# First half-step's entry taken from the features-on-partitions copy of x: norms by products with a column of ones

## Chip, cores and metric

The kernel runs on one core of one Trainium2 chip. The metric is the device time of one execution in microseconds (us); the median of several runs counts. TensorE is called PE (its weight loads PEld), VectorE DVE, ScalarE ACT, GpSimd POOL, and SyncE, whose queue issues most DMAs, SP.

## The reference

One decoder layer on x of 1024 tokens by 1024 features, all in float32, with a first SwiGLU half-step, a mixer (attention and pooling), a second half-step and a last norm:

```
h = x + 0.5 * swiglu(rms_norm(x, ffn1_norm), w1, w3, w2)
u = rms_norm(h, mix_norm);  proj = u @ w_in
h = h + (sigmoid(gA) * yA + sigmoid(gB) * yB) @ w_out
h = h + 0.5 * swiglu(rms_norm(h, ffn2_norm), ...)
out = rms_norm(h, final_norm)
rms_norm(x, g) = x * rsqrt(mean(x*x, axis=-1) + 1e-6) * g
swiglu(x, w1, w3, w2) = (silu(x @ w1) * (x @ w3)) @ w2
```

Only the start of the first half-step is touched: the norm of x and what is made of it for the products with w1 and w3 (1024 by 2816 each).

## The kernel before

**Products.** Each matrix product is split as Strassen and Winograd do it, with seven products of half-size blocks in place of eight. For a pair j of two 128-column strips of w1 (quad a) and of w3 (quad b), a quad runs the products m = 1, 6, 2, 7, 5, 4, 3. The normed x enters as seven operands of 512 features by 512 tokens: `b11`, `b21` (first 512 tokens, low and high features), `b22` (last tokens, high features), and four sums `t1` to `t4` of the blocks. m=1 uses b11, m=2 b21, m=6 t2, m=7 t3, m=5 t1, m=4 t4, m=3 b22. Every operand, of x and of the weights, is split into a higher part (ACT copies it to a shorter float format, fp32r) and a lower part (the difference, by DVE or POOL), and a product is 12 matmuls of 128x128 by 128x512: four blocks of features by three pairings of the parts (`Sevens.product`, L314). Weights come in 512 KB pieces (`raw`, L69) and are split by `Sevens.split` (L303 on ACT, L306 on POOL or DVE). Results leave PSUM through `a_out` and `b_out` (L473 and after).

**Operands of x.** The left operands need features on partitions. Before, x is loaded by rows, 128 tokens on partitions (`load_rows`, L769). Per row tile ACT squares and sums along the row (`squares`, L259), DVE and POOL make the inverse root (`inverse`, L263 and L264), DVE scales by it and by the gain (`scaled_part` L270, `scaled` L267), and `Rows` has PE transpose four 128x128 blocks into a PSUM bank (L381), ACT copy the higher part from it (L382) and DVE subtract for the lower part (`Rows.lower`, L385). For the last four row tiles `Entry.run` also makes t1, t2, t4 (DVE, L423 to L425) and t3 (POOL, L426) by rows and transposes all five. The gain is spread over partitions by widening it to columns (L808) and transposing (L814).

**Order.** `begin_up1` is under a manual schedule: each engine gets its instructions in the order in which the code records them. It runs 12 products, m=1 and m=2 of both quads for three pairs, first m=1 of pairs 0 and 1, while the rest of x is made ready between them; each takes its weights' split two products ahead (`operand(i + 2)`). `up` then runs m = 6, 7, 5, 4, 3 of those six quads, and after them the other pairs. `keep_on(n)` has PE multiply ones by ones into an unused bank (`idle`, L804) while it would stand. The loads of x and of the first weights share SP's queue, at most some eight in flight.

Of the kernel before, what the change touches and what calls it, by code (L numbers as in the profile page):

```python
# [126 lines left out]
def tile_block(  # L127
# [31 lines left out]
    def sbuf(name, side="left", bufs=1):  # L159
        return tc.tile_pool(name=name, bufs=bufs, side=side, reuse_waits="tile")  # L160
# [7 lines left out]
    def bank(tag, name):  # L168
        return psum.tile([P, HALF], F32, tag=tag, name=name)

    def tmp(name):
        return keep.tile([P, 1024], F32, tag="tmp", bufs=TMP_BUFS, name=name)

    def row(name):
        return keep.tile([P, 1024], F32, tag="raw", bufs=RAW_BUFS, name=name)

    def h_tile(name):
        return keep.tile([P, D], F32, tag="h", bufs=NT, name=name)
# [2 lines left out]
    consts.tile([P, 24], F32, name="pad")  # L181
    ident = consts.tile([P, P], F32, name="ident")
    ones = consts.tile([P, P], F32, name="ones")
    mhalf = consts.tile([P, 1], F32, name="mhalf")
    consts.tile([P, 32], F32, name="pad2")
    ve.memset(ones, 1.0)
    ve.memset(mhalf, -0.5)
    h = []
    h_dram = [[dram.tile([P, D], F32, name=f"h{i}_dram{t}") for t in range(NT)] for i in range(2)]

    def load_gain(src, name):
        t = keep.tile([P, D], F32, tag="gain", bufs=1, name=f"gain_{name}")
        nc.scalar.dma_start(t, src.to_broadcast([P, D]))
        return t

# [3 lines left out]
    def ffn_pieces(w1, w3, w2, ahead):  # L199


        order = [(j, w, i) for j in range(NPAIR) for w in (w1, w3) for i in range(2)]
        order.sort(key=lambda o: (o[2], o[0]) if o[0] < ahead else (2,))

        spare = lambda j, i: (h_tile,) if ahead == 3 and (j, i) == (0, 1) else ()
        raws.pieces += [(w[2 * j + i], (1024,), *spare(j, i)) for j, w, i in order]
        by = w2.rearrange("(j o p) c -> o p j c", o=2, p=P)
        for m in DOWN:
            for js in PAIRS:
                for k, n in m.loads:  # L210
                    raws.pieces.append((by[k][:, js, n * HALF:(n + 1) * HALF], (js.stop - js.start, HALF)))
# [45 lines left out]
    def squares(t, out):  # L257
        inv[t] = small.tile([P, 2], F32, tag="nst", name=f"nst_{t}")
        ac.activation(out, h[t], AF.Square, accum_out=inv[t][:, 0:1])  # L259
# [6 lines left out]
    def scaled(t, out, gain):  # L266
        ve.scalar_tensor_tensor(out, h[t], inv.pop(t)[:, 1:2], gain, op0=OP.mult, op1=OP.mult)  # L267

    def scaled_part(t, c, gain):
        ve.scalar_tensor_tensor(h[t][:, c], h[t][:, c], inv[t][:, 1:2], gain[:, c], op0=OP.mult, op1=OP.mult)  # L270

    def norm_rows(t, gain, name, alloc=row):
        y = alloc(f"hn_{name}{t}")
        squares(t, y)
# [7 lines left out]
    SUMS = ("t4", "b22", "b11", "t2", "b21", "t3", "t1")  # L282
    LOWS, HIGHS = slice(0, HALF), slice(HALF, S)

    def sums_of_x(pool, name, order, **kw):
        return {
            s: tuple(pool.tile([P, 4, HALF], F32R, name=f"x{part}_{s}_{name}", **kw) for part in ("hi", "lo"))
            for s in order
        }

    class Sevens:
# [14 lines left out]
            eng.tensor_tensor(w[:, 1], src, w[:, 0].bitcast(F32), op=OP.subtract)  # L306
            return w

        def product(self, p, w, x, start=True):
            hi, lo = self.X[x]  # L310
            for k in range(4):
                r = slice(k * P, (k + 1) * P)
                for q, (a, b) in enumerate(three((w[:, 0, r], w[:, 1, r]), (hi[:, k, :], lo[:, k, :]))):
                    pe.matmul(p, a, b, start=(start and k == 0 and q == 0), stop=(k == 3 and q == 2),  # L314
                              skip_group_check=not start)
# [3 lines left out]
    class Quad:  # L319
# [36 lines left out]
                ve.tensor_tensor(src, a12, self.s2, op=OP.subtract)  # L356
            self.w[m] = self.sv.split(src, f"{n}{m}", eng)

        def run(self, m, back=True):
            if m not in self.w:  # L360
                self.operand(m)
            w, n = self.w.pop(m), self.n
            x = {1: "b11", 2: "b21", 3: "b22", 4: "t4", 5: "t1", 6: "t2", 7: "t3"}[m]
            key = {1: "x", 2: "x", 5: "v", 3: "v"}.get(m, m)
            if m not in (2, 3):
                self.bank[key] = bank("mm" if key in ("x", "v") else "acc", f"u_{self.sv.name}{n}{m}")
            self.sv.product(self.bank[key], w, x, start=m not in (2, 3))
            if m == 3 and back:
                raws.back(2)
            return self.bank[key]  # L370
# [72 lines left out]
    class Pair:  # L443
# [3 lines left out]
        def __init__(self, sv, j, sums, early=False, spare=False):  # L447


            self.sv, self.j, self.sums = sv, j, sums  # L450
            self.place_of = [h_tile if spare else tmp, h_tile if early else tmp]
            self.u2 = (lambda n: h_tile(f"u2_{n}")[:, :HALF]) if spare else (lambda n: sv.half_tile("u", n))
            self.y = []
            self.A, self.B = Quad(sv, f"{j}a"), Quad(sv, f"{j}b")
            self.u = {}
# [303 lines left out]
    ac.activation(warm, mhalf, AF.Silu)  # L759

    scope = ExitStack()
    X = sums_of_x(scope.enter_context(sbuf("x1")), "f1", SUMS)

    for t in range(NT):
        h.append(h_tile(f"x{t}"))

    def load_rows(*ts):
        for t in ts:
            nc.sync.dma_start(h[t], x[t * P:(t + 1) * P, :])  # L769

    gain_row = keep.tile([P, D], F32, tag="gain", bufs=1, name="gain_ffn1")
    square = row("square")
    columns_tile = tmp("columns")
    columns = columns_tile.rearrange("p (k c) -> p k c", k=KT)

    def load_all():
        nc.scalar.dma_start(ident, c_ident)
        load_rows(0, 1, 2, 3)
        raws.depth = 2
        raws.load()  # L780
        load_rows(4)
        raws.depth = 3
        raws.load()
        load_rows(5)
        raws.depth = 4
        raws.load()
        load_rows(6, 7)
        raws.depth = 6
        raws.load()

    def pre_run(sv, todo, first, low):
        return Entry(sv, [(*((q.A, m, q.a_out), (q.B, m, q.b_out))[k],) for q, m in todo for k in range(2)], low,
# [2 lines left out]
    def begin_up1():  # L795


        load_all()
        idle = bank("mm", "idle")

        def keep_on(n):

            for _ in range(n):
                pe.matmul(idle[:, :P], ones, ones, start=True, stop=True)  # L804

        def widen(b):
            k = slice(4 * b, 4 * b + 4)
            ve.tensor_copy(columns[:, k], gain1[:, k, None].to_broadcast([P, 4, P]))  # L808

        def gains(b):  # L810

            p = bank("acc", f"gain{b}")
            for k in range(4):
                pe.transpose(p[:, k * P:(k + 1) * P], columns[:, 4 * b + k], ident)  # L814
            return p

        r = {}

        def rows(t, what, c):
            scaled_part(t, c, gain_row)  # L820
            r[t] = Rows(X, what, h[t][:, c], t)

        keep_on(12)
        widen(0)
        squares(0, square)
        widen(1)
        inverse(0)
        g = [gains(b) for b in range(2)]
        keep_on(2)
        ve.tensor_copy(gain_row[:, LOWS], g[0])  # L830
        squares(1, square)
        squares(2, square)
        rows(0, "b11", LOWS)
        inverse(1)
        keep_on(2)
        inverse(2)
        squares(3, square)
        rows(1, "b11", LOWS)
        r[0].lower()
        keep_on(3)  # L840
        rows(2, "b11", LOWS)
        inverse(3)
        r[1].lower()
        keep_on(3)
        pairs = [Pair(sv1, j, sums, True, j == 2) for j in range(3)]
        entry = pre_run(sv1, [(q, m) for m in (1, 2) for q in pairs[:2]] + [(pairs[2], m) for m in (1, 2)],
                        pairs[0], h[:4])
        entry.operand(0)
        rows(3, "b11", LOWS)
        r[2].lower()  # L850
        keep_on(2)
        r[3].lower()
        ve.tensor_copy(gain_row[:, HIGHS], g[1])
        entry.product(0)
        entry.operand(1)

        square2 = columns_tile
        squares(4, square2)
        for t in (0, 1):
            rows(t, "b21", HIGHS)  # L860
        entry.product(1)
        entry.out(0)
        entry.operand(2)
        entry.operand(3)
        inverse(4)
        r[0].lower()
        for t in (2, 3):
            rows(t, "b21", HIGHS)
            r[t - 1].lower()
        entry.product(2)  # L870
        entry.out(1)
        squares(5, square2)
        r[3].lower()
        entry.product(3)
        entry.operand(4)
        entry.out(2)
        entry.operand(5)
        entry.out(3)

        def high(t, part):  # L880
            if part == 0:
                inverse(t)
                return
            scaled(t, h[t], gain_row)
            return h[t]

        def after(t):
            if t + 2 < NT:
                squares(t + 2, square2)
            if t == 5:  # L890
                raws.depth = 8
                raws.load()

        entry.run(high, after, 4)
        return pairs

    sums = spilled("f1")
# [1249 lines left out]
```

## Time and profile before

| | us |
|---|---|
| median of 3 runs | 1937.25 (1936.93 to 1937.53) |
| the profiled execution | 1938.85 |
| its span, first to last instruction | 1937.1 |
| first matmul of the first product | 14.06 |
| first matmul on b21 (fifth product) | 27.86 |
| first matmul with m=6 (quad a of pair 0) | 59.68 |
| first matmul of quad b of pair 0 with m=6 | 75.05 |
| first matmul of pair 3 | 143.4 |

A line of a group or of the timeline names the engine, the line of the kernel, the operation, the tiles (out<-in) and shapes; in the timeline the first two numbers are start and duration in us, and xN means that N like instructions are merged, the duration from the first's start to the last's end. What stands in brackets is the engine's idle time before, and who ended it. In a table of stretches each engine has its busy time and (x) the number of its instructions. A matmul's recorded duration contains its pipeline's depth, so records of matmuls overlap: 12 of a product are recorded at 0.39 each and take 2.73 together.

### The profile page before, as it was taken

The numbers are of one execution on the slowest core, as the hardware profiler recorded it, in microseconds if no ns is written. First come the engines' busy times: TensorE is split into PE (matmuls) and PEld (weight loads), VectorE is DVE, ScalarE is ACT, GpSimd is POOL, SyncE is SP. The second block draws the span as 40 slices with busy tenths as digits, with TensorE's granted clock in tenths as the row PEclk, the third lists the DMA queues.
The fourth block names the chain that finished last, engine by engine and source line by source line (L and its number), as shares of the span: only waits on it lengthen the run. The fifth ranks groups of instructions, "written<-read, shape, count | busy, mean of one in ns | idle before, by whom it ended". The sixth has DMA issues, their size and how long they took to land.

```text
span 1937.1 us, 24938 instructions
## 1 busy us (share of the span) xinstructions
PE 1906.0 (98%) x8938; PEld 1574.9 (81%) x8938; DVE 1347.7 (70%) x2012; ACT 759.3 (39%) x1361; POOL 741.2 (38%) x557
## 2 busy tenths in 40 slices
PE   9999999999999999999999999999999999999997
PEld 7788888887888888888877888887888888878885
DVE  7786556658676876658775896787665566577776
ACT  6333333333344543334445762353333333333343
POOL 5433333332222355445544356543333333322231
PEclk9999999999999999999999999999999999999998
DMA  4154222336465538665668877733433233364654
GB/s 187 44 195 167 90 87 104 136 114 212 146 235 208 197 99 257 219 207 198 217 232 303 279 226 248 271 133 118 165 121 114 82 105 123 121 206 136 205 199 150
DMA packets 144796, 331.98 MB, mean 171 GB/s; under 512 B 19104, under 2 KB 39840, under 8 KB 143136
## 3 DMA queue, kind: packets, MB, share of 16 engines
q1 hardware_dynamic: 137136, 308.00, 46.4%
q10 hardware_dynamic: 7536, 22.39, 3.4%
q8 instruction: 70, 1.15, 0.3%
q14 instruction: 54, 0.44, 0.1%
HBM read 229.61 MB, written 100.73 MB: 171 GB/s over the span
## 4 chain that ended last, share of the span: by engine, by line
PE 39%; DVE 4%; issue 3%; POOL 2%; ACT 2%; DMA 1%; DVEq 0%; POOLq 0%; ACTq 0%
PE d_f L708 7%; PE wo L1870 4%; PE u_mixm L314 2%; PE yp L1626 2%; PE o L1572 1%; PE u_f210a L314 1%; PE u_f29b L314 1%; PE u_f29a L314 1%; PE u_f28b L314 1%; PE u_f28a L314 1%; PE u_f27b L314 1%; PE u_f27a L314 1%; PE u_f26b L314 1%; PE u_f26a L314 1%; PE u_f25b L314 1%
## 5 line engine op out<-in xcount | busy, mean ns | idle before, releaser
L708 PE MATMUL d_f<-bhi_f,alo_f 128*128 128x512 f32 x616 | 240.8, 391 | 2.5 <-POOL alo_f L670 2.1
L708 PE MATMUL d_f<-bhi_f,ahi_f 128*128 128x512 f32 x616 | 240.6, 391 | 0.2 <-ACT ahi_f L666 0.2
L708 PE MATMUL d_f<-blo_f,ahi_f 128*128 128x512 f32 x616 | 239.7, 389 | 0.0
L670 POOL TENSOR_TENSOR alo_f<-g_f,ahi_f 128x512 fp32r<-128x512 f32 x70 | 99.0, 1430 | 299.5 <-ACT ahi_f L666 299.5
L314 PE MATMUL u_mixm<-xhi_t_mix,wc_mixm 128*128 128x512 f32 x608 | 195.3, 392 | 1.8 <-POOL wc_mixm L306 1.7
L314 PE MATMUL u_mixm<-xhi_b_mix,wc_mixm 128*128 128x512 f32 x456 | 149.1, 392 | 1.2 <-ACT y_m L972 0.9
L708 PEld LDWEIGHTS d_f<-bhi_f,alo_f 128*128 128x128 f32 x616 | 115.6, 188 | 29.6 <-POOL alo_f L670 4.0
L314 PEld LDWEIGHTS u_mixm<-xhi_t_mix,wc_mixm 128*128 128x128 f32 x608 | 113.8, 188 | 27.3 <-POOL wc_mixm L306 3.8
L708 PEld LDWEIGHTS d_f<-bhi_f,ahi_f 128*128 128x128 f32 x616 | 115.6, 188 | 24.2 <-ACT ahi_f L666 0.6
L708 PEld LDWEIGHTS d_f<-blo_f,ahi_f 128*128 128x128 f32 x616 | 115.7, 188 | 23.8
L314 PE MATMUL u_mixm<-xlo_t_mix,wc_mixm 128*128 128x512 f32 x304 | 118.4, 390 | 0.0
L306 POOL TENSOR_TENSOR wc_mixm<-s_mixm,wc_mixm 128x512 fp32r<-128x512 f32 x52 | 74.4, 1433 | 108.1 <-ACT wc_mixm L303 104.1
L314 PEld LDWEIGHTS u_mixm<-xhi_b_mix,wc_mixm 128*128 128x128 f32 x456 | 85.6, 188 | 19.5 <-ACT y_m L972 1.3
L303 ACT ACTIVATE wc_mixm<-s_mixm 128x512 fp32r<-128x512 f32 x76 | 47.3, 629 | 126.5 <-DVE s_mixm L347 63.3
L314 PE MATMUL u_mixm<-xlo_b_mix,wc_mixm 128*128 128x512 f32 x228 | 88.8, 389 | 0.0
L666 ACT ACTIVATE ahi_f<-g_f 128x1024 fp32r<-128x1024 f32 x84 | 81.9, 975 | 4.0 <-DMA g_f<-gs_f 3.9
L306 POOL TENSOR_TENSOR wc_mixm<-raw,wc_mixm 128x512 fp32r<-128x512 f32 x40 | 61.0, 1530 | 34.6 <-ACT wc_mixm L303 32.1
L666 ACT ACTIVATE bhi_f<-s_f2w 128x512 fp32r<-128x512 f32 x55 | 32.8, 627 | 97.9 <-DVE s_f2w L686 87.0
L1870 PE MATMUL wo<-w_o,o_hi 128*128 128x512 f32 x224 | 69.3, 391 | 0.0
L666 ACT ACTIVATE bhi_f<-s_f1w 128x512 fp32r<-128x512 f32 x55 | 33.0, 630 | 86.8 <-DVE s_f1w L686 82.0
L314 PEld LDWEIGHTS u_mixm<-xlo_t_mix,wc_mixm 128*128 128x128 f32 x304 | 57.1, 188 | 11.8 <-DVE xlo_t_mix L385 0.2
L670 DVE TENSOR_TENSOR alo_f<-g_f,ahi_f 128x1024 fp32r<-128x1024 f32 x42 | 51.3, 1222 | 7.3 <-ACT ahi_f L666 7.3
(1302 smaller groups left out, 5103.8 us busy)
## 6 DMA issues: line engine op xcount, KB each, us to landing
g_f<-gs_f SPq DMA_DIRECT2D x70, 512.0 KB, 4.5
gs_f<-y_f SPq DMA_DIRECT2D x88, 256.0 KB, 3.0
raw<-in_w2a_dram SPq DMA_DIRECT2D x35, 512.0 KB, 3.7
raw<-in_w2b_dram SPq DMA_DIRECT2D x35, 512.0 KB, 4.6
gs_f<-gb_f SPq DMA_DIRECT2D x46, 256.0 KB, 2.2
raw<-in_w1a_dram SPq DMA_DIRECT2D x22, 512.0 KB, 4.8
raw<-in_w3a_dram SPq DMA_DIRECT2D x22, 512.0 KB, 5.5
raw<-in_w1b_dram SPq DMA_DIRECT2D x22, 512.0 KB, 4.3
```

The costliest lines, as they stand in the source:

```text
L303: ac.activation(w[:, 0], src, AF.Copy)
L306: eng.tensor_tensor(w[:, 1], src, w[:, 0].bitcast(F32), op=OP.subtract)
L314: pe.matmul(p, a, b, start=(start and k == 0 and q == 0), stop=(k == 3 and q == 2), skip_group_check=not start)
L666: ac.activation(hi[:, c], src, AF.Copy)
L670: eng.tensor_tensor(lo[:, d], src[:, o], hi[:, d].bitcast(F32), op=OP.subtract)
L708: pe.matmul(self.banks[m][t], l, r, start=(first and q == 0), stop=(last and q == 2))
L1572: pe.matmul(p, l, r, start=(j == 0), stop=(j == end))
L1626: pe.matmul(p, a, b, start=(j == 0), stop=(j == 11))
L1870: pe.matmul(banks[m][t], l, r, start=(st == 0 and j == 0 and q == 0), stop=(st == 1 and j == 1 and q == 2))
```

## The change

x is taken from a copy that lies in memory with features on partitions, in two halves of 512 tokens, each in four tiles of two blocks of 128 features. ACT squares such a tile (`square`), its two blocks are added (`add`: on DVE for the first half, on POOL for the second), and `count` multiplies the sum by a column of ones on PE, four products of one column, so that PSUM gathers the sum of squares with tokens on partitions. `inverses` makes the inverse roots (DVE, POOL), widens them to 128 columns on DVE, and has PE transpose them: a PSUM bank `by_token` then holds the inverse root of each of the 512 tokens on all partitions. `normed` multiplies a block by the gain (now one number per partition) and by that bank, in place. ACT copies the higher part and DVE subtracts for the lower part, both from SBUF. The sums t1 to t4 are made by blocks of features on blocks that already lie as they are used; `Rows`, `Entry.run` and their transposes are no longer used here (they stay for the later entries). Products 0 and 1 are run alternately, one block of features at a time. The squares and the widened columns use the places of operands not yet made (t4, b22, t3). One piece of weights more is loaded ahead (depth 7), and two temporary tiles of pair 2 lie elsewhere (`place_of`, `u2`).

```diff
-    X = sums_of_x(scope.enter_context(sbuf("x1")), "f1", SUMS)
...
+    x_in = [[h_tile(f"x{half}_{j}").rearrange("p (r c) -> p r c", r=2) for j in range(KT // 2)] for half in range(2)]
...
-        load_rows(0, 1, 2, 3)
...
+        load_x(0, 0, 1, 2, 3)
+        load_raws(2)
+        load_x(1, 0, 1)
+        load_raws(3)
+        load_x(1, 2)
+        load_raws(4)
+        load_x(1, 3)
+        load_raws(7)
...
+        def square(half, j):
+            ac.activation(place(half, j), x_in[half][j], AF.Square)
+
+        def add(half, j, eng):
+            t = place(half, j)
+            eng.tensor_tensor(t[:, 0], t[:, 0], t[:, 1], op=OP.add)
+
+        def count(half, j):
+
+            t = place(half, j)
+            for q in range(4):
+                pe.matmul(sums_of[half][:, q:q + 1], t[:, 0, q * P:(q + 1) * P], ones[:, 0:1],
+                          start=(j == 0 and q == 0), stop=(j == 3 and q == 3), skip_group_check=True)
+
+        def inverses(half):
+
+            st = small.tile([P, 8], F32, tag="nst8", name=f"nst_x{half}")
+            ve.tensor_scalar(st[:, :4], sums_of[half][:, :4], 1.0 / D, EPS, op0=OP.mult, op1=OP.add)
+            gp.tensor_tensor(st[:, 4:], st[:, :4], mhalf4, op=OP.pow)
+            wide = wides[half][:, 0, :].rearrange("p (q c) -> p q c", q=4)
+            ve.tensor_copy(wide, st[:, 4:, None].to_broadcast([P, 4, P]))
+            by_token[half] = bank("acc", f"inverses{half}")
+            for q in range(4):
+                pe.transpose(by_token[half][:, q * P:(q + 1) * P], wide[:, q], ident)
...
+        def normed(half, k):
+            b = block(half, k)
+            ve.scalar_tensor_tensor(b, b, gain1[:, k:k + 1], by_token[half], op0=OP.mult, op1=OP.mult)
...
+        def lower(what, k, src):
+            hi, lo = X[what]
+            ve.tensor_tensor(lo[:, k, :], src, hi[:, k, :].bitcast(F32), op=OP.subtract)
...
+        keep_on(10)
+        for j in range(4):
+            square(0, j)
+            add(0, j, ve)
+            count(0, j)
+            keep_on(2 if j < 3 else 3)
+        inverses(0)
...
+        operand(0)
+        operand(1)
+        for k in range(4):
+            split("b11", k)
+        lower("b11", 3, block(0, 3))
+        for k in range(4):
+            for i in (0, 1):
+                product(i, range(k, k + 1))
+        operand(2)
+        out(0)
+        square(1, 0)
+        add(1, 0, gp)
+        operand(3)
+        out(1)
+        square(1, 1)
+        add(1, 1, gp)
+        split("b21", 4)
+        split("b21", 5)
+        square(1, 2)
+        add(1, 2, gp)
+        split("b21", 6)
+        square(1, 3)
+        add(1, 3, gp)
+        split("b21", 7)
+        lower("b21", 3, block(0, 7))
+        product(2)
+        for j in (0, 1):
+            count(1, j)
+        out(2)
+        product(3)
+        for j in (2, 3):
+            count(1, j)
+        operand(4)
+        inverses(1)
+        operand(5)
+        out(3)
...
+        def first_sums(k):
+            normed(1, k)
+            normed(1, k + 4)
+            ve.tensor_tensor(b11(k), b12(k), b11(k), op=OP.subtract)
+            ve.tensor_tensor(t2(k), b22(k), b11(k), op=OP.subtract)
+            gp.tensor_tensor(b12(k), b22(k), b12(k), op=OP.subtract)
+            higher("t2", k, t2(k))
+            if k > 0:
+                lower("t2", k - 1, t2(k - 1))
...
+        def last_sums():
+            both("t1", b11)
+            for k in range(4):
+                ve.tensor_tensor(b21(k), t2(k), b21(k), op=OP.subtract)
+            X.update(sums_of_x(x1, "f1", ("t4",)))
+
+        beside = [lambda k=k: first_sums(k) for k in range(4)]
+        beside += [lambda: (lower("t2", 3, t2(3)), both("t3", b12)), last_sums,
+                   lambda: both("t4", b21, (0, 1)), lambda: both("t4", b21, (2, 3))]
+        for i in range(4, n):
+            product(i)
+            beside[i - 4]()
+            operand(i + 2)
+            out(i)
...
+        both("b22", b22)
```

`split(what, k)` is `normed(0, k)`, `higher`, and the lower part of the block before; `both` is higher and lower for the named blocks.

## The prediction

> **What bounds the kernel now.** I read the page first, for the engines over the whole span and the granted clock.
>
> ```profile
> span 1937.1 us, 24938 instructions
> PE 1906.0 (98%) x8938; PEld 1574.9 (81%) x8938; DVE 1347.7 (70%) x2012; ACT 759.3 (39%) x1361; POOL 741.2 (38%) x557
> PEclk9999999999999999999999999999999999999998
> ```
>
> PE is busy almost throughout at full clock, so what an entry takes or gives in PE time goes to the end undiminished. Next I cut the table of busy time by stretches at the events that the change moves: first product (14.05), first product on `b21` (27.86), first product of a quad's second part, m=6 (59.65), the same of the b-quad (75.05), start of the fourth pair (143.40).
>
> ```profile
> core 0: us, PE busy (x) PEld busy (x) DVE busy (x) ACT busy (x) POOL busy (x), PEclk, DMA share, GB/s
> 0.00:14.05 14.05, 11.10 (x72) 10.06 (x72) 6.77 (x17) 8.81 (x16) 3.33 (x9) 1.00 0.89 343
> 14.05:27.86 13.81, 13.09 (x64) 10.58 (x64) 11.58 (x16) 8.60 (x16) 7.41 (x7) 1.00 0.57 227
> 27.86:59.65 31.79, 31.47 (x177) 26.29 (x176) 27.95 (x37) 18.83 (x36) 21.17 (x15) 1.00 0.16 51
> 59.65:75.05 15.40, 14.42 (x62) 10.96 (x61) 11.32 (x15) 5.90 (x11) 5.62 (x5) 1.00 0.20 52
> 75.05:143.40 68.35, 68.35 (x302) 56.42 (x301) 55.40 (x69) 18.93 (x32) 23.28 (x17) 1.00 0.45 150
> ```
>
> The last stretch holds 25 products: 68.35 / 25 = 2.73 us each, PE never idle, DVE 81% busy. From 65 us on the list of waits has none of PE's up to 420. So the change is worth the shift of the instant 75.05, and nothing later makes up for it. In 27.86 to 59.65 DVE is 88% and POOL 67% busy: they are close behind PE. How these two get along is in the timeline:
>
> ```profile
> start us, us, engine line op out<-in xcount [idle before <-releaser]
> 25.37 0.69 DVE L423 TENSOR_TENSOR x<-x,x 128x512 f32<-128x512 f32 x1
> 25.54 1.68 POOL L306 TENSOR_TENSOR wc_f10a<-raw,wc_f10a 128x512 fp32r<-128x512 f32 x1 [1.82 <-PE u_f11a L314]
> 26.09 1.67 DVE L424 TENSOR_TENSOR s_f1t<-x,x 128x512 f32<-128x512 f32 x1
> 27.17 1.74 POOL L306 TENSOR_TENSOR wc_f10b<-raw,wc_f10b 128x512 fp32r<-128x512 f32 x1
> 27.79 1.67 DVE L425 TENSOR_TENSOR s_f1t<-s_f1t,x 128x512 f32<-128x512 f32 x1
> ...
> 33.90 2.26 POOL L306 TENSOR_TENSOR wc_f11b<-raw,wc_f11b 128x512 fp32r<-128x512 f32 x1
> 35.28 1.29 DVE L385 TENSOR_TENSOR xlo_t_f<-x_t,xhi_t_f 128x512 fp32r<-128x512 f32 x2 [0.26 <-ACT xhi_t_f L382]
> ```
>
> L424 and L425 take 0.69 us alone (as L423) and 1.67 beside POOL; POOL's 1.28 becomes 1.68 and 1.74. Each ends 0.55 (DVE) or 1.15 (POOL) after the other: they take turns. But the lower halves L385, which read PSUM, run two in 1.29 inside POOL's instruction. So a DVE operation with both inputs in SBUF costs up to 1.0 more beside POOL, one with an input in PSUM nothing.
>
> **What the change takes and adds.** Removed from PE: 112 transposes of x and 8 of gains (16 take 34.02 to 35.68, 0.10 each: about 12 us). Added: 32 products with a column of ones, 8 transposes. From ACT: 8 squares with their accumulator read (0.19) become 8 without. From DVE: 28 lower halves from PSUM become 28 with both inputs in SBUF. That is the step I price highest. Loads have equal size and places in the queues, so I take the landings of before: x at 4.4, 5.9, 7.2, 8.5 (squares start there), weights after.
>
> I lay the new order out engine by engine with these rows: product 2.73; ACT square 1.06, copy 0.52 in a row, 0.60 alone; DVE 0.61 in a row, 0.69 alone; POOL 1.28; POOL's power 0.55. A column-of-ones product is not in the trace. A 128x128 one of `idle` is two records, 0.10 each in a row, hence 0.2; if only its weights counted it could be half. I take 0.2, four make 0.8.
>
> *To product 2.* The last square ends at 9.5, add 10.2, counts 11.2, DVE and the power 12.0. The widening copy (0.38, L808) now stands beside a POOL split that begins at 12.0; no row shows a copy there. Bounds: 0.4 and, by L424, 0.4 + 1.1. I take the upper end: 13.6. The Trainium skill, SBUF — State Buffer, "Who interferes with whom", says that copies can enter a mode that holds the port pair shared with GpSimd, the other fully blocking; by it both widening copies wait, as I have them. Transposes, norm (0.74, L270), ACT copy: first product at 15.7, where 14.06 was. Its second matmul waits for the lower half, and products 0 and 1 alternate by blocks: 24 matmuls at 0.228 (2.73 / 12) and 0.5 of waiting. Product 2 starts at 21.7; before 22.54. Gain 0.8.
>
> *To product 4.* Product 2 ends at 24.4. PE then counts the second half's squares, and every later product stands behind that in its queue. Its cover in the first half was loading; here it is one chain over four engines. ACT: an eviction at 21.2, square at 21.7, weights' copy, eviction, square at 23.7; POOL: add, split, add, to 26.6; PE counts, product 3 from 27.5 to 30.2. Behind two copies of `b21` ACT squares at 25.8, and behind a third that waits for DVE at 28.4; POOL's add (delayed 0.5 by a lower half) ends at 31.3, counts 32.3, DVE 32.5. The power stands behind a split on POOL (31.3 to 33.0), so 33.5; widening copy 35.0, transposes: product 4 at 35.5, before 27.86. Loss 7.6.
>
> *To m=6.* Now DVE has, in one queue ahead of the operand of m=6: 8 norms from PSUM (0.64), 2 evictions (0.61), and with both inputs in SBUF 8 differences, 4 lower halves of t2, 4 of t3, 4 of t1, 4 differences for t4, 2 lower halves of t4, and the two sums of weights: 28 x 0.61. That is 5.1 + 1.2 + 17.1 = 23.4, and some 0.5 of dependences. POOL has 10 operations in that time (6 splits, 4 differences); with 28 of 38 DVE operations exposed about 7 meet one, at 1.0: 7. DVE ends at 35.8 + 30.9 = 66.7, ACT copies, m=6 starts at 67.4; before 59.68. The eight products between need 21.9 and wait 4.8 for weights' splits that stand on POOL behind differences and blocked turns, so they end at 62.2 and PE stands: what it saves in transposes disappears under a longer DVE queue. Loss 7.7 in all at this point.
>
> *m=6, 7, 5, 4, 3.* Before, 15.4 for 13.7 of products. After, weights are split just before use (0.9 twice before a third matmul), the lower half for m=5 stands behind four of `b22` on DVE (1.3), and m=3 waits 1.1 for its split on POOL: 13.7 + 4.2 = 17.9. The b-quad starts at 85.3; before 75.05. Laid out so, before's own rows give 75.3, so I take off 0.2: **+10.0 us**. If the two widening copies wait for nothing it is +8; if all ten POOL operations are met, +13.
>
> The profiled execution took 1938.85 (span 1937.1 and 1.75 around it): 1948.9. It lies 1.6 above the median of the runs, 1937.25, so the forecast is 1947.3.
>
> **Rivals.** *PE stays the bound (faster).* If the second half's norms and sums are ready whenever PE wants them, products 2 to 11 take 27.3 from 21.7, with 3.2 of counting (16 at 0.2) and 0.4 of transposes: m=6 at 52.6, 7.1 earlier, and 1930. For it: PE loses 12 us of work and DVE has 12% idle before. Against: it decides only if DVE's 38 operations ahead of m=6, 23.4 us even undisturbed, end by 52, so begin by 28.5, and by the chain above the second half's last square is not done before 29. Chance 0.08.
>
> *The port is no loss (same).* If DVE's operations on SBUF alone pass POOL as those from PSUM do, its queue ahead of m=6 is 24 us and begins 3 earlier (two copies at 1.1, the adds): it ends at 56.8, m=6 starts about 2 earlier than before, and the waits behind it, which stay longer, leave -1.3: 1936. L424, L425 and L267 (1.28 alone, 2.34 beside POOL) speak against. With results between that and +3.9, 0.12.
>
> *Longer still.* PE stands for 3.0 us before product 4 and 5.2 before m=6. The first 24 records of `idle`, after a standing start, took 4.81 us, 0.20 each, against 0.10 later. If the waits bring that back, some 24 records again at double cost are 2.4 each time; most would lie under the waits named above. With the worst meeting of POOL this makes +13 to +15, 1950 to 1952. The Trainium skill, TensorE: Matmul & The Clock Gate, part 1, has the clock halve after about 3.4 us without work; the second wait is longer than that, the first is not. No row of before has such a wait in mid-kernel. Chance 0.20.
>
> **Numbers.** The forecast's own case, +6 to +12.5, has 0.60. A measurement of this kernel can tell about 0.2% (3.9 us) from no change: slower 0.60 + 0.20 = 0.80, same 0.12, faster 0.08. The range takes the forecast's case, the longer one and a little of the half-hidden port: 1940 to 1953.
>
> **What would show it.** Right: PE idle ahead of the inverses' transposes of the second half by about 3 us and ahead of u_f10a m=6 by about 5; DVE over 95% busy from 36 to 66 us with lower halves of 1.6 to 1.8 us beside POOL's splits; u_f13a starting near 153 instead of 143.4; nothing changed behind it but the shift. Wrong: lower halves of 0.69 us beside POOL, PE without gaps from 16 to 60 us, or m=6 before 60 us.

## The result: 19 us slower

The changed kernel takes 1956.13 us (median of 4 runs, 1955.18 to 1956.55), the one before 1937.09 beside it: a ratio of 1.0097, 95% interval 1.008 to 1.0115. The forecast was 1947.3 with a range to 1953: the sign was right, the time lies above the range. The profiled execution took 1956.07, span 1954.3. The page of the changed kernel, engines and granted clock:

```profile
span 1954.3 us, 24784 instructions
PE 1913.3 (98%) x8886; PEld 1580.4 (81%) x8886; DVE 1356.5 (69%) x2012; ACT 759.5 (39%) x1353; POOL 746.3 (38%) x555
...
PEclk7999999999999999999999999999999999999999
```

PE has 52 matmul records fewer than before and 7.3 us more busy time, and the first slice of the clock row, 9 before, is 7. That is the first hint at what the forecast lacked. The table of stretches of the changed kernel, cut at the same events (first product, product 4, m=6, quad b of pair 0, pair 3):

```profile
core 0: us, PE busy (x) PEld busy (x) DVE busy (x) ACT busy (x) POOL busy (x), PEclk, DMA share, GB/s
0.00:20.15 20.15, 16.39 (x80) 15.48 (x81) 6.01 (x11) 7.63 (x10) 3.86 (x7) 0.69 0.92 362
20.15:44.22 24.07, 19.42 (x85) 16.04 (x85) 12.60 (x16) 12.14 (x19) 12.85 (x9) 0.78 0.07 27
44.22:76.58 32.36, 25.37 (x98) 18.94 (x96) 30.92 (x38) 13.78 (x26) 17.15 (x10) 0.92 0.05 17
76.58:95.00 18.42, 17.26 (x61) 12.96 (x62) 14.14 (x18) 8.79 (x16) 7.33 (x6) 0.83 0.22 72
95.00:163.10 68.10, 68.10 (x301) 56.22 (x300) 55.46 (x69) 18.93 (x32) 23.01 (x17) 1.00 0.48 166
```

Column PEclk is full in the last stretch alone. That stretch takes 68.10 where 68.35 were in the table of before (68.15 from the first matmul of its quad b, at 75.28): nothing behind 95 us has changed but the shift, which is 19.7 at its end (163.1 against 143.4). Against the forecast's instants:

| us | before | forecast | after |
|---|---|---|---|
| first product | 14.06 | 15.7 | 20.15 |
| product 4 | 28.08 | 35.5 | 44.22 |
| m=6 | 59.68 | 67.4 | 76.58 |
| quad b of pair 0 | 75.28 | 85.3 | 95.0 |
| pair 3 | 143.4 | 153.6 | 163.1 |

The tables ahead of this section have 27.86 and 75.05 for product 4 and quad b; those are the last matmuls of the products before them, and the first of their own are at 28.08 and 75.28. The forecast is 4.45 short at the first product and 8.7 short at product 4; from there on the gap stays within 1.0 (9.2 at m=6, 9.7 at quad b, 9.5 at pair 3). PE's list of waits in the first 165 us:

```profile
PE u_f10a L314 <- ACT wc_f10a L303: 5.1, 1, 5.1
PE inverses L845 <- DVE wide L842: 4.2, 2, 2.9
PE squares L833 <- POOL squares_b22hi L827: 1.8, 1, 1.8
...
PE u_f10a L314 <- DVE y_f L484: 1.0, 1, 1.0
```

The columns are total, times, longest. The waits before m=6 (5.1) and before the second half's transposes (2.9) are the two that the prediction asked for. In the first, ACT's copy of the weights is named; ACT itself had stood 3.36 us for DVE's sum of weights `s_f10a` (L347), the last of DVE's queue, at 75.81. What the port does is in the timeline at 49 us:

```profile
49.29 1.67 DVE L945 TENSOR_TENSOR sum<-x,x 128x512 f32<-128x512 f32 x1
...
50.37 1.74 POOL L946 TENSOR_TENSOR x<-x,x 128x512 f32<-128x512 f32 x1
...
50.88 1.78 DVE L859 TENSOR_TENSOR xlo_t_f<-sum,xhi_t_f 128x512 fp32r<-128x512 f32 x1
```

A lower half whose inputs both lie in SBUF takes 1.78 beside POOL, as forecast. So the missing 9 us lie earlier, and PE's timeline there shows them:

```profile
7.68 1.87 PE L833 MATMUL squares<-ones,squares_t4hi 128*128 128x1 f32 x8
9.40 1.20 PE L814 MATMUL idle<-ones 128*128 128x128 f32 x4
...
12.96 1.71 PE L833 MATMUL squares<-ones,squares_t4lo 128*128 128x1 f32 x8
```

In the kernel before, four records of `idle` take half of that:

```profile
7.08 0.61 PE L804 MATMUL idle<-ones 128*128 128x128 f32 x4
```

Four counts (x8, two records each) take 1.71 to 1.87 and four records of `idle` 1.20. In the narrow run of study 6, which has the clock full there, they take 0.95 and 0.69. From 7.7 to 24.8 us the granted clock of the changed kernel is 0.50, though PE is busy 15.50 of these 17.10 us. It falls again from 34.5 to 38.2 us (0.55), behind the wait of 1.8 between the second half's counts.

### The profile page after: what moved, and what is told of

Its sections match the earlier page's. It is cut to its first block, busy times and chain, and to the rows that moved or that the text cites. A ratio compares the mean times of both kernels' runs of the same rounds, so it can differ in the third digit from the quotient of the medians.

```text
span 1954.3 us, 24784 instructions
## 1 busy us (share of the span) xinstructions
PE 1913.3 (98%) x8886; PEld 1580.4 (81%) x8886; DVE 1356.5 (69%) x2012; ACT 759.5 (39%) x1353; POOL 746.3 (38%) x555
## 5 line engine op out<-in xcount | busy, mean ns | idle before, releaser
L672 DVE TENSOR_TENSOR blo_f<-raw,bhi_f 128x1024 fp32r<-128x1024 f32 (+1 forms) x24 | 30.6, 1273 | 37.8 <-ACT bhi_f L668 37.8
```

Of the source, the lines that this page charges most:

```text
L672: eng.tensor_tensor(lo[:, d], src[:, o], hi[:, d].bitcast(F32), op=OP.subtract)
```

## Experiments

Theory in short, as it stood ahead of these runs: of the 19 us, ten are what was forecast (late chain, port), and nine come from a halved clock ahead of product 4; study 9 makes these nine 7.3. The rivals differ by study. The instants given (first product, product 4, m=6) are those of one profiled execution of each kernel; "ratio" is to the kernel before, run on the same chip, with its 95% interval.

**1. Counts 128 columns wide** (`e1_wide_counts`).

```diff
-                pe.matmul(sums_of[half][:, q:q + 1], t[:, 0, q * P:(q + 1) * P], ones[:, 0:1],
+                pe.matmul(sums_of[half][:, q * P:(q + 1) * P], t[:, 0, q * P:(q + 1) * P], ones,
...
```

> The changed kernel, but each product of a square with ones takes all 128 columns of ones in place of one (the first column is read); number and order of instructions are the same. Theory A, products of one column do not count as work for TensorE's clock: the granted clock, half from 7.7 to 24.8 us in the changed kernel, stays full there; counts, copies and transposes and products 0 and 1 run at full rate, the first product starts near 16.2 us (20.15 in the changed kernel), product 4 near 38.5 (44.2), m=6 near 69 to 71 (76.6), and the time is about 1948 to 1950 us, some 7 below the changed kernel. Theory B, the clock falls because TensorE waits for other engines between the counts (the chain square, add, count): the columns make no difference, the first product stays within 0.5 of 20.2 us and the time within 1.5 of 1956.

Measured: 1952.06 us, ratio 1.0068 (1.0051 to 1.0085); first product 18.54, product 4 41.45, m=6 73.76. Between the two theories. PE still waited 2.2 and 0.8 before product 0, and matmuls were at half rate from 18.5 to 24.1. So the width seems to matter and the waits too; this run alone does not part them (studies 5 to 7 do).

**2. POOL without the t3 differences** (`e2_no_t3_diff`).

```diff
-            gp.tensor_tensor(b12(k), b22(k), b12(k), op=OP.subtract)
```

> The changed kernel without GpSimd's four differences for t3 (t3 is then made of the normed b12 alone; four operations on GpSimd left out, nothing else). Theory A, VectorE and GpSimd take turns on operands in SBUF: each of the four takes about 1.1 us from VectorE's queue between product 4 and m=6, so m=6 starts 3 to 4.5 us earlier, at 72 to 73.5 us against 76.6, and the time is about 1952 to 1953. Theory B, VectorE's queue is long by its own 38 operations and GpSimd only happens to be busy beside it: m=6 stays within 0.7 us of 76.6, the time within 1 of 1956.

Measured: 1955.58 us, ratio 1.0089 (1.0074 to 1.0104); m=6 at 75.25. DVE's queue ahead of m=6 became 29.7 long, from 31.2: 1.5 for four of POOL's ten operations. By its time this is theory B's case (within 1 of 1956); by m=6, 1.3 earlier, it lies between the two. It left open whether the price per meeting is small or the other six now meet more.

**3. One half's inverses for both** (`e3_one_inverse`).

```diff
-        square(1, 0)
-        add(1, 0, gp)
...
-            count(1, j)
...
-        inverses(1)
+        by_token[1] = by_token[0]
```

> The changed kernel without the second half's squares, adds, counts, inverse roots and their transposes: the second half of x is scaled by the first half's inverse roots. Nothing before product 2 changes (first product at 20.2 us). Theory A, the second half's chain over four engines is what delays product 4: product 2 follows 1 and 3 follows 2 with waits for weights' splits alone, product 4 starts near 35 to 36 us (44.2 in the changed kernel), m=6 near 67 to 68 (76.6), the time about 1947 to 1948. Theory B, the time behind product 4 is set by VectorE's queue whatever the chain does, because that queue is full before: product 4 comes earlier, but m=6 by less than 4 us, and the time is 1952 or more.

Measured: 1949.65 us (1946.06 to 1951.18), ratio 1.0057 (1.0042 to 1.0072); product 4 at 36.27 and m=6 at 69.04, 8.0 and 7.5 earlier, though the first product started 1.6 later (21.73). What is gained ahead of product 4 is kept almost in full at m=6, since the chain lies ahead of DVE's queue, as theory A had it; the time is 1.65 above theory A's. Its first product is late in the same code because the clock stayed low longer there: transposes took 1.12 and matmuls 0.63 up to about 27 us.

**4. The operand of m=6 first** (`e4_m6_first`): the lower halves of t1 and b22 go behind m=6.

```diff
...
-        beside += [lambda: (lower("t2", 3, t2(3)), both("t3", b12)), last_sums,
-                   lambda: both("t4", b21, (0, 1)), lambda: both("t4", b21, (2, 3))]
+        beside += [lambda: (lower("t2", 3, t2(3)), both("t3", b12)), lambda: highers("t1", b11),
+                   lambda: None, lambda: (lowers("t1", b11), highers("b22", b22))]
+        later.extend([last_sums, lambda: None, lambda: lowers("b22", b22)])
...
```

> The changed kernel with the same instructions in another order on ScalarE and VectorE: the sums of weights that m=6 waits for go ahead of the lower parts of t1, of t4 and of b22, which are then made between the first products of up. Theory A, the shared port's total work is the bound (all of VectorE's and GpSimd's operations up to m=3 have to pass in turns): the wait of 5.1 us ahead of m=6 goes away, m=6 starts near 71 to 72 us against 76.6, but a wait of 4 to 6 us appears ahead of the last products of the a-quad, the b-quad's m=6 starts within 2 us of 95.0, and the time is 1954 to 1956. Theory B, the wait ahead of m=6 is only a matter of what stands ahead of it in the queue: the b-quad starts 4 to 5 us earlier, at 90 to 91, and the time is 1951 to 1952.

Measured: 1956.61 us, ratio 1.0097 (1.0082 to 1.0112). m=6 starts at 69.83, 6.75 earlier (1.56 of it lay already ahead of product 4, at 42.66), and quad b at 94.58, 0.4 earlier. Its list of PE's waits begins with

```profile
PE u_f10a L314 <- DVE y_f L484: 7.4, 1, 7.4
```

The wait of 5.1 at m=6 is gone and one of 7.4 at m=3 has come. As theory A had it, the total of DVE's work is what binds here, not its order (the time is 0.6 above theory A's).

**5 and 6. Waits filled, counts wide or narrow** (`e5_wide_filled`, `e6_narrow_filled`): `idle` products stand in every long wait; the second has the counts of the change.

```diff
...
-        keep_on(10)
+        keep_on(18)
...
-            keep_on(2 if j < 3 else 3)
+            keep_on(2 if j < 3 else 13)
...
-        keep_on(3)
+        keep_on(6)
...
+                keep_on(8, by_token[1])
...
+        keep_on(13, by_token[1])
...
+        keep_on(22, bank("mm", "idle6"))
```

> The kernel of e1 (products with all 128 columns of ones) with more products of ones by ones in TensorE's queue wherever the changed kernel's TensorE waits: 8 more at the start, 10 more ahead of the first half's transposes, 3 more behind them, 8 and 13 around the second half's counts, 22 ahead of m=6. Nothing else is touched. Theory A, what the prediction missed is the clock alone (the granted clock falls where TensorE stands or has only thin work, and the work behind it then runs at half rate): the clock stays full from 5 us to the end, first product at 16 to 16.5 us (20.15 in the changed kernel), product 2 near 22, product 4 near 36, m=6 near 67.5 (76.6), the b-quad's m=6 near 85.5 (95.0), the time 1946 to 1948 us, which is the prediction's own sum. Theory B, the added products only take TensorE's time and the clock follows something else: the time stays at 1950 or more.

> As e5_wide_filled, but the products that count the squares have one column again, as in the changed kernel. Theory A1, products of one column do not count as work for the clock, even with others between them: half clock appears around the counts at 6 to 12 us, the first product comes 2 to 4 us later than in e5_wide_filled and the time is 1949 to 1952. Theory A2, only the waits count: within 1 us of e5_wide_filled at the first product and 1 us in the time.

Measured: wide 1950.84 us, ratio 1.0069 (1.0052 to 1.0085), first product 17.39, m=6 70.13; narrow 1951.35, ratio 1.0072 (1.0057 to 1.0087), 18.99 and 71.69. The wide run misses theory A (1946 to 1948) and has theory B's time, although the clock is full from its first count up to 53 us. The narrow run lies between A1 and A2. With the waits filled, narrow counts cost 1.6 at the first product; the 0.5 between the medians is no more than the spread of the runs. The 1.6 is a half-clock spell from 12.6 to 16.0 us (26 `idle` records in 4.78 against 3.07). No wait of PE lies ahead of it. Both runs have a flaw: 18 `idle` products at the start run over 1 us past the first add, so the first count begins at 7.3 to 7.5 instead of 6.1. The wide one shows how long a spell is; its stretches:

```profile
50.00:53.20 3.20, 1.61 (x7) 1.00 (x7) 3.17 (x5) 1.16 (x3) 2.21 (x3) 1.00 0.00 0
53.20:56.60 3.40, 3.40 (x10) 2.52 (x8) 3.40 (x4) 2.74 (x6) 3.28 (x2) 0.51 0.01 2
56.60:60.00 3.40, 3.40 (x16) 2.52 (x15) 3.40 (x4) 3.40 (x7) 1.88 (x2) 0.99 0.15 34
```

Two waits of 0.69 and 0.90 leave PE half busy for 3.2 us (1.61), and the next 3.4 us run at a granted clock of 0.51, with 10 records instead of 16. The Trainium skill, TensorE: Matmul & The Clock Gate, Part 1, has the clock set by activity in free-running windows of about 3.4 us. The length agrees. The page's spell follows an idle window of that length; here waits of 1.6 us in sum came ahead of it. The same two waits stand in the narrow run, 1.5 us later (0.69 and 0.90), and there no spell follows: matmuls stay at 0.39. So such waits can bring a spell and need not.

**7. The kernel before with `idle` products of one column** (`e7_before_narrow_idle`), which isolates the width.

```diff
-                pe.matmul(idle[:, :P], ones, ones, start=True, stop=True)
+                pe.matmul(idle[:, :1], ones, ones[:, 0:1], start=True, stop=True)
```

> The kernel before, with one edit: the 24 products of ones by ones that fill TensorE's waits up to the first product have one column in place of 128. Nothing of its work is changed. Theory A1, products of one column do not count as work for the clock: full clock begins later than 5 us, the gains' and the first row tiles' transposes are recorded at double length (0.2 each in place of 0.1), the first product starts later than 14.06 us by 0.5 to 2, products 0 and 1 run partly at half rate, and the time is 2 to 4 us above before. Theory A2, only waits count: clock and milestones as before, time within 1 us of 1937.

Measured: 1941.4 us against 1937.78, ratio 1.0019 (1.001 to 1.0029). First product 16.56 instead of 14.06, pair 3 at 148.0 instead of 143.4. PE's timeline of this kernel:

```profile
1.05 5.28 PE L804 MATMUL idle<-ones 128*128 128x1 f32 x24 [1.05 <-DVE mhalf L187]
...
9.11 1.11 PE L381 MATMUL x_b<-ident,x 128*128 128x128 f32 x4
...
20.01 0.63 PE L314 MATMUL u_f10a<-xlo_b_f,wc_f10a 128*128 128x512 f32 x1
```

The transposes took 0.66 in the kernel before and take 1.11; matmuls take 0.63, not 0.39, until 21.7 us. After its start, PE waits for nothing longer than 0.5 there. So one-column products fill PE's records but do not raise the clock, as theory A1 had it (the first product is 0.5 later than its range). This is shown without any part of the change in the kernel.

**8. POOL emptied in the stretch** (`e10_no_pool`): no t3 differences, and the lower parts of the weights of products 6 to 11 are plain copies on ACT.

```diff
+            if eng == "copy":
+                ac.activation(w[:, 1], src, AF.Copy)
...
-            todo[i][0].operand(todo[i][1], gp)
+            todo[i][0].operand(todo[i][1], "copy" if 6 <= i < n else gp)
...
-            gp.tensor_tensor(b12(k), b22(k), b12(k), op=OP.subtract)
```

> The changed kernel with GpSimd emptied in the stretch between product 4 and m=6: its four differences for t3 are left out (t3 is made of the normed b12), and the lower parts of the weights of products 6 to 11 are left out as differences (ScalarE writes a plain copy in their place). VectorE's own work is untouched. In the changed kernel VectorE's queue from the first norm of the second half to the end of m=6's operand sums took 31.2 us (44.6 to 75.8), 29.7 in e2_no_t3_diff. Theory A, the port (the prediction's 7 us): with GpSimd empty the queue falls to its own rows, 24 to 25 us, m=6 starts about 6 us earlier than 76.6, near 70 to 71, and the time is 1949 to 1951. Theory B, the length is VectorE's own (e2's four operations were worth 0.4 each): the queue stays at 27.5 or more and the time at 1952 or more.

Measured: 1953.93 us, ratio 1.0084 (1.0068 to 1.0101); m=6 at 72.76. DVE's queue ahead of m=6, as one stretch each, in the changed kernel:

```profile
44.60:75.81 31.21, 24.99 (x96) 18.56 (x95) 30.92 (x38) 13.10 (x24) 17.15 (x10) 0.94 0.05 18
```

and with POOL emptied:

```profile
44.49:71.99 27.50, 24.35 (x96) 18.70 (x95) 24.21 (x38) 16.23 (x30) 0.00 (x0) 0.93 0.06 20
```

The same 38 DVE operations are busy 30.92 beside ten of POOL and 24.21 beside none: the port costs 6.7, the forecast had 7. The queue is only 3.7 shorter, since DVE then stands 3.3, most of it for PE (1.44) and ACT (0.46 and 1.10). In study 2 they were busy 28.89: four operations fewer gave 2.0 and the other six 4.7, 0.5 and 0.8 each. That answers what study 2 left open: the price is there, but an operation taken away does not return all of its own. By its queue (27.5) and its time the run is theory B's case; by what DVE's operations took it is theory A's.

**9. Waits filled to measure** (`e11_filled_tuned`): as the wide one of 5, with 12 `idle` products at the start and four ahead of each of products 8 and 9.

```diff
-        keep_on(10)
+        keep_on(12)
...
+            if i in (8, 9):
+                keep_on(4, by_token[0])
```

> e5_wide_filled with its fill put right: 6 products of ones fewer at the start (there the first count came 0.6 to 1.1 us late behind them) and 4 ahead of each of products 8 and 9 (their waits for weights, 1.6 us close together, were followed by 3.4 us at half clock from 53.2). Theory A, the clock and my own fill are all that parts e5_wide_filled from the prediction's sum: product 0 at 16.5 to 17, m=6 at 68 to 68.5 (70.1), no half clock behind 8 us, and the time 1947.5 to 1949. Theory B, other terms of the sum are short too: 1950 or more.

Measured: 1950.06 us (1949.66 to 1950.66), ratio 1.0063 (1.0048 to 1.0078). Its stretches, cut as above from product 4 on:

```profile
0.00:37.05 37.05, 35.59 (x236) 32.48 (x237) 18.64 (x26) 19.79 (x28) 16.77 (x16) 1.00 0.55 215
37.05:69.28 32.23, 30.36 (x160) 24.36 (x158) 30.89 (x38) 13.67 (x26) 17.10 (x10) 1.00 0.06 17
69.28:87.68 18.40, 15.12 (x60) 10.98 (x61) 14.14 (x18) 8.80 (x16) 7.32 (x6) 1.00 0.24 72
```

From the first count on the clock is full, and the durations agree (four records of `idle` 0.61, transposes 0.66, matmuls 0.39). Product 4 starts 7.2 earlier than in the changed kernel (44.22 - 37.05), and m=6, quad b and pair 3 are earlier by 7.3 each. So the clock is worth 7.3 in these profiles, 6.1 in the medians, and all of it ahead of product 4: the two later stretches take 32.23 and 18.40 at full clock, 32.36 and 18.42 at 0.92 and 0.83. By its time the run lies 0.06 on theory B's side of the line, and m=6 at 69.28 is later than theory A's 68 to 68.5: other terms of the sum are short too.

**10. The second half squared and counted early** (`e12_early_half`), without its adds, waits filled at the start, ahead of the first transposes and ahead of m=6.

```diff
-        load_x(1, 0, 1)
-        load_raws(3)
-        load_x(1, 2)
-        load_raws(4)
-        load_x(1, 3)
+        load_x(1, 0, 1, 2, 3)
...
-            for q in range(4):
...
+            for r in range(half + 1):
+                for q in range(4):
...
+        count(1, 0)
```

> e5_wide_filled with the second half's norm taken early: its tiles are loaded ahead of the weights of products 2 to 5, squared while ScalarE waits, counted without adds (eight products of ones for a tile in place of four), and its inverse roots stand ready behind product 2. What follows is as in the changed kernel: 38 operations of VectorE ahead of m=6. Theory A, by the prediction's own sum the second half's chain costs 7 to 8 us and VectorE's queue the rest: the queue begins near 31 us (38 to 39 in e5_wide_filled), m=6 starts near 64 (70.1), the b-quad near 82 and the time is 1943.5 to 1945.5; what is left over the kernel before is the queue. Theory B, an earlier queue meets more of GpSimd's splits and of PE's results: m=6 gains less than 4 us and the time is 1947 or more.

Measured: 1945.49 us (1944.94 to 1945.75), ratio 1.0039 (1.0024 to 1.0054); product 4 at 33.99, m=6 64.94. This is the upper end of theory A's 1943.5 to 1945.5: against study 9, taking the chain of squares, adds, counts, power and copy early is worth 4.3 at m=6. What then remains over before is DVE's queue: from 31.42 to 64.16 DVE is busy 32.46 of 32.74 us, and m=6 follows.

**11. Sums t1 and t2 written to PSUM** (`e13_sums_in_psum`), on top of 10, with the operand of m=6 ahead of the other sums, and ACT's copies and the evictions in another order.

```diff
-        sum2 = place_of_sum("t4", "lo", "sum2")
+        s1, s2 = bank("acc", "sum1"), bank("acc", "sum2")
...
-            ve.tensor_tensor(b11(k), b12(k), b11(k), op=OP.subtract)
-            ve.tensor_tensor(t2(k), b22(k), b11(k), op=OP.subtract)
+            ve.tensor_tensor(s1, b12(k), b11(k), op=OP.subtract)
+            ve.tensor_tensor(s2, b22(k), s1, op=OP.subtract)
+            ve.tensor_tensor(b21(k), s2, b21(k), op=OP.subtract)
```

> All of the change's arithmetic, rearranged by what the runs so far showed: as e12_early_half, and t1 and t2 are written into two PSUM banks, so that t2, t4 and the lower parts of t1 and t2 have one operand in PSUM (16 of VectorE's operations no longer with both in SBUF); copies of weights and evictions ahead of the sums in ScalarE's order, m=6's operand ahead of the lower parts of t3, t4 and b22, and the counts of the second half between the blocks of products 0 and 1. Theory A, port and order are what is left: the queue of VectorE has few operations of 1.6 to 1.8 us, TensorE waits under 5 us in all between product 0 and the b-quad, m=6 starts at 55 to 57 us (59.7 before), the b-quad at 72.5 to 74.5 (75.05 before), and the time is 1934.5 to 1937.5, not slower than the kernel before. Theory B, PSUM gives no relief or the waits bring half clock back: 1940 or more.

Measured: 1936.39 us (10 runs, 1934.97 to 1938.11) against 1937.89, ratio 0.9993 (0.9984 to 1.0002). m=6 starts at 56.39, 8.5 earlier than in 10. How much of this is PSUM and how much the new order (lower halves of t3, t4 and b22 now stand behind m=6's operand) was not measured apart. Its timeline at 36 us:

```profile
36.03 1.29 POOL L306 TENSOR_TENSOR wc_f11a<-raw,wc_f11a 128x512 fp32r<-128x512 f32 x1 [2.27 <-ACT wc_f11a L303]
36.10 0.70 DVE L949 TENSOR_TENSOR sum<-x,sum 128x512 f32<-128x512 f32 x1
...
36.83 0.69 DVE L950 TENSOR_TENSOR x<-sum,x 128x512 f32<-128x512 f32 x1
...
40.01 1.30 POOL L951 TENSOR_TENSOR x<-x,x 128x512 f32<-128x512 f32 x1
...
40.52 1.34 DVE L948 TENSOR_TENSOR sum<-x,x 128x512 f32<-128x512 f32 x1
```

L949 and L950 have one input in PSUM and take 0.70 and 0.69 inside POOL's instructions, which take 1.29 as if alone. L948 has both in SBUF: begun at 40.52 while POOL runs to 41.31, it takes 1.34. Writing to PSUM does not save it; reading from there does. The Trainium skill, SBUF — State Buffer, "Who interferes with whom", says that two SBUF inputs contend with a GpSimd instruction that reads SBUF, and one does not. The trace agrees.

**12. Adds back on POOL, widening copy later** (`e14_adds_back`): tiles 2 and 3 of the second half are added again, so they need half the counts.

```diff
+                add(1, 2 + k // 2, gp)
...
-        inverses(1)
+        st = inverses_begin(1)
...
+        widen(1, st)
```

> e13_sums_in_psum with two edits: tiles 2 and 3 of the second half are added on GpSimd again (16 products of ones in place of 32 for them), and the widening copy goes behind the last norm of b21, so that VectorE does not stand while GpSimd takes the power. Theory A, what bounds e13 up to m=6 is the start of VectorE's queue (29.35 us there): it starts near 28.4, m=6 at 55.3 to 56 (56.4), the b-quad at 72.9 to 73.4 (73.95), and the time is 1935.3 to 1936.0, 0.4 to 1.1 below e13's 1936.4 and 0.1 per cent below the kernel before. Theory B, the adds on GpSimd meet VectorE's lower parts of b11 and b21 and give it back: 1936.4 or more.

Measured: 1935.6 us (11 runs, 1934.82 to 1936.99) against 1936.98, ratio 0.9994 (0.9985 to 1.0003). Pair 3 starts at 140.72, 1.2 earlier than in 11 and 2.7 earlier than before. The ratio does not tell it from 11, nor either from the kernel before. Its time is the one that theory A gave, 20 us below the change as given.

## Why the prediction was right in sign and short in size

- *The failed step: pricing all of PE's work up to product 4 at full clock, the counts first ("I take 0.2, four make 0.8").* At full clock the 0.8 is right: from the start of four counts to the next record it is 0.81 with one column (study 6) and 0.89 to 0.99 with 128 (study 9). In the changed kernel it is 1.56 to 1.72, the transposes take 1.11 in place of 0.66 and the first matmuls 0.63 in place of 0.39, since the clock is halved there. That is 3.65 of the 4.45 that the forecast is short at the first product (16.50 in study 9), and 7.2 of the 8.7 at product 4. Two things bring it: one-column products leave the clock at half rate (study 7), and half-rate spells stand behind waits even with wide counts (study 1). At product 4 wide counts alone take back 2.8 (41.45), filled waits alone 4.8 (39.45), both together 6.3 (37.91) or, tuned, 7.2 (37.05). These are single profiles, and the change's own code up to there spans 42.66 to 44.39 (after, studies 2, 4 and 8), so the two shares are rough.
- *"Longer still" had the right mechanism in the wrong place.* It put a halved clock behind the waits of 3.0 and 5.2 before product 4 and m=6 and priced it at 2.4 each, mostly hidden. What cost time was the clock halved from the first half's counts into the midst of products 0 and 1, and again in product 3 (4.42 in place of 2.84, behind the wait of 1.8 for POOL's add); it was worth 7.3. Behind the two long waits the clock did fall (0.50 from 44.2 to 48.0, 0.83 from m=6 to quad b), and there it cost next to nothing (32.36 against 32.23, 18.42 against 18.40): "most would lie under the waits named above" held.
- *To product 2.* The widening copy of 1.48 is the upper bound that was taken (1.5); in study 10 it runs with POOL standing and takes 0.43. The power is a term that was mis-sized: 0.55 was read from a tile of 128x1, and the one of 128x4 took 1.02. With full clock the first product is at 16.50, 0.8 over the forecast: 0.47 of power, and 0.3 of counts, which end at 11.5 there in place of 11.2.
- *To product 4.* At full clock 37.05 against 35.5. Product 2 is 0.9 over (22.62), product 3 1.5 (28.98): 0.9 is product 2's lateness, passed on by ACT's first square (22.63, forecast 21.7), and 0.5 is POOL's second add, which took 1.76 beside a lower half of DVE in place of 1.28. The wait before the second half's transposes was 2.87, forecast 3.0.
- *To m=6.* The best of the steps: DVE's queue was 31.2 long, forecast 30.9; the wait of PE 5.05, forecast 5.2; the port 6.7 (study 8), forecast 7. In the wait there is some luck: the eight products ahead of it were busy 25.4 with 1.9 of waits for splits, where 21.9 and 4.8 were forecast, because half clock took the place of waits. The port's price is not what emptying POOL would return, however: only 3.7 came back.
- *m=6, 7, 5, 4, 3.* 18.4 against 17.9. The wait of 1.0 at m=3 was in the sum, with the wrong releaser: it is DVE's `y_f`, not POOL's split.
- *The sum.* At full clock the change costs 12.4 at pair 3 (155.8 - 143.4), 2.2 over the forecast. The rest of 19.7, 7.3, is the clock.
- *The rivals.* "PE stays the bound" falls with the 5.1 and 2.9 of waits, "the port is no loss" with the 1.78. Study 11 shows what both would have needed: sums read from PSUM and the second half's norms early. PE then stands for 2.2 in all for POOL's splits at `u_f10a`, in place of 5.1 at m=6.

What stays open: what the clock counts as activity. One column does not raise it and 128 do; widths between, and how many wide products among narrow ones are enough, were not tried. Nor do the runs tell when a short wait brings a spell (study 5). The first product came at 18.96 to 21.73 in five profiles of kernels that are alike up to there (after, studies 2, 3, 4, 8), so up to 2.8 us of its lateness depend on the execution.

## What to carry to other kernels

Products that only keep PE occupied should be wide (128 columns did here what one did not), and a new chain of small products needs to be priced at half clock until a row shows otherwise. Where an edit turns a PSUM input of DVE into an SBUF one, count the operations that POOL runs beside it and charge a full turn for each meeting. Writing the intermediate to PSUM, where it is read again, took that turn away here; taking work off POOL returned 3.7 of 6.7. Where the queue that makes a late operand has no gaps, another order in it only moves the wait (study 4); starting it earlier or making it shorter helped (studies 10 and 11).

## What the runs showed of the hardware that was not expected

- Products of 128x128 by one column: 24 records in a row, two for each product, took 5.28 us at the start, against 4.81 for 128 columns, and left the clock at half rate until 21.7 us (study 7).
- The clock row can miss a half-rate spell: in studies 3 and 7 it shows 1.00 where transposes take 1.11 in place of 0.66 and matmuls 0.63 in place of 0.39. The duration of one known form is the safer reading.
- Two waits of 1.6 us in sum within 3.2 us stood ahead of a spell of half clock of 3.4 us in the wide run of study 5; in the narrow one the same two waits had no spell behind them.
- POOL's power took 0.55 on 128x1 and 1.02 on 128x4, with nothing of DVE beside it.
